# A hybrid decoder layer on one core: the input projection by pairs of column tiles, with the last 128 tokens held still

## The chip, the cores and the metric

The kernel runs on one core of a Trainium2 chip. The metric is device time in microseconds (us) of one launch, as the median of several runs. The engines are named as in the profile: PE is TensorE (PEld its weight loads, which overlap its matmuls), DVE is VectorE, ACT is ScalarE, POOL is GpSimd, and SP is SyncE, which only issues DMAs here. Each engine works through its own instructions in program order; a DMA that an engine issues stands in that order too.

## The reference, cut to what matters

One inference step of a decoder layer for 1024 prompt tokens and 8 x 8 sample tokens, 1088 tokens in all, 2048 features. All tensors are float32.

```
h = x @ w_in + b_in            # (1088 x 2048) @ (2048 x 9984); columns are split into q, k, v, gates
oa = banded_attention(rope(qa), rope(ka), va, window 128, sinks)      # 16 heads
ob = combine over g of banded_attention(rope(q_g), rope(k_g), v_g, dilation 1, 4, 16)   # 8 heads each
ya, yb = oa * silu(za), ob * silu(zb)
m = sigmoid(g_a) * (ya @ w_br_a) + sigmoid(g_b) * (yb @ w_br_b)
y = LayerNorm(alpha * x + m @ w_out)
# also returned: the key/value windows of the prompt and the updated caches of the samples
```

## The kernel before, in words

Every product is made from two float32r parts of each operand, `hi` (the rounded value, a cast on ACT) and `lo` (the rest, a subtraction on DVE): hi x hi, lo x hi and hi x lo, so three matmuls where one stood. `x` is held transposed in the on-chip memory for the whole projection: 16 tiles `xhi[k]`, `xlo[k]` of 128 features x 1088 tokens. The 9984 columns of `w_in` are 78 column tiles of 128.

`in_proj` makes one column tile after the other (the first two together). The weights of a tile are the matmul's stationary side (128 x 128) and the tokens move past them in three chunks, `CHUNKS`, of 384, 384 and 320. For each of four groups of four k-tiles the chunks are taken in turn. That is 16 k x 3 chunks x 3 products = 144 matmuls for a tile, each with a weight load of its own. After its last k a chunk is evacuated by `evac` from PSUM to SBUF with the bias. PSUM has eight banks, four under the tag `d` (`psd()`), where the projection accumulates, and four under `a` (`psa()`), for everything else.

`Weights` loads `w_in` in raw pieces of 512 KB over SP's queue (`wraw`, two buffers), and splits each into two parts of 512 columns (`whi` on ACT, L89; `wlo` on DVE, L90), three parts ahead of the one in use.

The first 34 tiles are q, k and v (`evac_qkv`: rotary on DVE, casts one tick later, stores to DRAM over POOL's queue). The last 44 are the gates z and g (`evac_z`, L954): ACT writes a `z` buffer of which there are two, and SP stores it to DRAM one tick later (L956).

The order of the work beside the matmuls is written by hand: a `tick()` stands after each chunk of a group (12 in a column tile). It first runs what `after(n, f)` had put off, and during the last 44 tiles it then takes a number of steps of a generator, `beside()`: attention (333 steps), decode (111), and `merge` (67), which multiplies the attention results by their weights and by silu(z). `RATES` says how many steps a tick takes in each. In `merge`, an item is one of 12 row tiles of `y`: a step loads `num` (L841, over SP), `w` and `z` (L844, L847, over POOL's queue), DVE multiplies (L854 to L859), ACT takes the sigmoid `sg` (L865), DVE gates (L866, L867), and ACT issues the store of `y` (L890) from the `z` buffer, of which `merge` has two. Items 0 to 7 take 4 steps each, items 8 to 11 take 8. After the projection come the branch and output products (L1019 to L1068), which read `y` back.

Of the kernel before, what the change touches and what calls it, by code (L numbers as in the profile page):

```python
# [10 lines left out]
F32 = mybir.dt.float32  # L11
# [8 lines left out]
P = 128  # L20
# [15 lines left out]
CHUNKS = ((0, 384), (384, 768), (768, T))  # L36
ALPHA = 2.0 ** 0.25
# [14 lines left out]
ORDER = [9] + [n for n, f in enumerate(FT) if f[0] in "qkv" and n != 9]  # L52
ORDER += [n for k in "zg" for n, f in enumerate(FT) if f[0] == k]

# [51 lines left out]
def layer_kernel(ctx: ExitStack, tc: tile.TileContext, A, O, S):  # L106
# [6 lines left out]
    masks = const.tile([P, 4, P], F32, tag="masks", name="masks")  # L113
# [8 lines left out]

    srcs = [tuple(A["w_in"][n, :, 512 * h:512 * (h + 1)] for n in ORDER[:2]) for h in range(4)]
    srcs += [A["w_in"][n, :, 1024 * h:1024 * (h + 1)] for n in ORDER[2:] for h in range(2)]
# [39 lines left out]
    def in_proj(batches, g0, evac, tick):  # L164
        for fts in batches:
            def product(w, i, c, k):
                a, b = CHUNKS[c]
                h, l = (t[:, k % 4 * P:(k % 4 + 1) * P] for t in w)
                o = pts[i][c][:, :b - a]
                nc.tensor.matmul(o, lhsT=h, rhs=xhi[k][:, a:b], start=(k == 0), stop=False)  # L170
                nc.tensor.matmul(o, lhsT=h, rhs=xlo[k][:, a:b], start=False, stop=False)  # L171
                nc.tensor.matmul(o, lhsT=l, rhs=xhi[k][:, a:b], start=False, stop=(k == KT - 1))  # L172

            for kg in range(4):
                if kg == 0:
                    pts = [[psa() if i == 1 and c else psd() for c in range(3)] for i in range(len(fts))]
                if kg == 0 and g0 == 0:

                    ws = [W.get(i) for i in range(2)]
                    g0 = 2  # L180
                    for k in range(4):
                        for i in range(2):
                            for c in range(3):
                                product(ws[i], i, c, k)
                        tick()
                    continue
                for i, ft in enumerate(fts):
                    if g0 < 6:
                        next_x(2)
                        W.load_to(4)  # L190
                    W.ahead(g0)
                    if g0 == 5:
                        constants()
                    w = W.get(g0)
                    g0 += 1
                    for c, (a, b) in enumerate(CHUNKS):
                        for k in range(4 * kg, 4 * kg + 4):
                            product(w, i, c, k)
                        if kg == 3:
                            evac(ft, c, a, b, pts[i][c])  # L200
                        tick()
# [8 lines left out]
    with tc.tile_pool(name="qp", bufs=2, side="right") as qp:  # L210
# [25 lines left out]
        def constants():  # L236
            nc.sync.dma_start(out=bias, in_=A["b_in"])
            for t, n in ((cost, "cost"), (sint, "sint"), (ident, "ident"), (masks, "masks")):
                nc.sync.dma_start(out=t, in_=A[n])
# [10 lines left out]
        for k in range(8):  # L250
            next_x()
            W.split_to((1, 2, 2, 2, 3, 4, 4, 4)[k])
            W.load_to(1 + (k > 1) + (k > 5))
# [12 lines left out]
        def evac_qkv(ft, c, a, b, pt):  # L266
            kind, idx, dil = FT[ft]
            n, e = b - a, min(b, NT)
            m = e - a
            bcol = bias[:, ft:ft + 1]  # L270
            if kind == "v":
                if c == 0:
                    held["f"] = qp.tile([P, T], F32, tag="kv", name="kvf", bufs=3)
                f = held["f"]
# [7 lines left out]
            raw = qp.tile([P, 384], F32, tag="raw", name="raw")  # L282
            sw = qp.tile([P, 384], F32, tag="sw", name="sw")
            nc.scalar.activation(raw[:, :n], pt[:, :n], AF.Identity, bias=bcol)  # L284
            nc.vector.stream_shuffle(sw[:, :n], raw[:, :n], SWAP)
            nc.vector.tensor_mul(raw[:, :n], raw[:, :n], cost[:, a:b])
            nc.vector.tensor_mul(sw[:, :n], sw[:, :n], sint[:, a:b])
            if c == 0:
                held["hi"] = qp.tile([P, NT], F32R, tag="hi", name="qhi", bufs=1)
                held["lo"] = qp.tile([P, NT], F32R, tag="lo", name="qlo", bufs=1)  # L290
                if kind == "k":
                    held["f"] = qp.tile([P, T], F32, tag="kv", name="kvf", bufs=3)
            hi, lo, f = held["hi"], held["lo"], held.get("f")
            if kind == "q":
                nc.vector.tensor_add(raw[:, :n], raw[:, :n], sw[:, :n])  # L295
                src = nat(raw, dil, m)
            else:
                src = cm(f, dil, a, e)
# [4 lines left out]
            def split():  # L303
                nc.scalar.copy(cm(hi, dil, a, e), src)
                nc.vector.tensor_tensor(out=cm(lo, dil, a, e), in0=src, in1=cm(hi, dil, a, e).bitcast(F32),
                                        op=ALU.subtract)
                if e < b:
                    after(3, store)

            def store():  # L310
                if kind == "q":
# [946 lines left out]
```

## Time and profile before

| | us |
|---|---|
| median of 3 runs | 2760.76 |
| lowest, highest | 2759.12, 2764.41 |
| the profiled execution: its own time | 2763.79 |
| the profiled execution: span from first to last instruction | 2761.8 |

The durations below are those of the profiled execution, 3.0 us above the median of the runs. The span holds five stretches: the start (0 to about 20 us), the rest of the q, k and v tiles (to 829 us), the gate tiles with attention and decode beside them (to about 1880 us) and with `merge` beside them (to 2082 us), and the two closing products. A timeline row gives the start, the duration, the engine, the line and the operation; what stands in square brackets is the idle time before it and what ended that.

### The profile page before, as it was taken

The numbers are of one execution on the slowest core, as the hardware profiler recorded it, in microseconds if no ns is written. First come the engines' busy times: TensorE is split into PE (matmuls) and PEld (weight loads), VectorE is DVE, ScalarE is ACT, GpSimd is POOL, SyncE is SP. The second block draws the span as 40 slices with busy tenths as digits, with TensorE's granted clock in tenths as the row PEclk, the third lists the DMA queues.
The fourth block names the chain that finished last, engine by engine and source line by source line (L and its number), as shares of the span: only waits on it lengthen the run. The fifth ranks groups of instructions, "written<-read, shape, count | busy, mean of one in ns | idle before, by whom it ended". The sixth has DMA issues, their size and how long they took to land.

```text
span 2761.8 us, 43516 instructions
## 1 busy us (share of the span) xinstructions
PE 2727.9 (99%) x16643; PEld 2625.8 (95%) x16643; DVE 1477.8 (54%) x2648; ACT 928.5 (34%) x1857; POOL 855.2 (31%) x905
## 2 busy tenths in 40 slices
PE   8999999999999999999999999999999999999997
PEld 8999999999999999999999998889999989988986
DVE  5444442443436777777665432124555556855866
ACT  4122222222223444444433332223224434433442
POOL 1112122131126666677677723433110000000001
PEclk9999999999999999999999999999999999999999
DMA  7345454464464333454445534657876745754763
GB/s 227 102 129 178 161 183 156 142 203 153 161 222 126 113 113 109 129 151 145 145 146 147 149 102 155 198 186 220 277 243 232 245 129 172 235 187 137 244 221 99
DMA packets 206088, 467.64 MB, mean 169 GB/s; under 512 B 28936, under 2 KB 128648, under 8 KB 203128
## 3 DMA queue, kind: packets, MB, share of 16 engines
q1 hardware_dynamic: 167512, 312.33, 35.8%
q0 software_dynamic: 36272, 145.19, 16.7%
q10 hardware_dynamic: 2096, 7.34, 0.7%
q8 instruction: 131, 2.15, 0.3%
q14 instruction: 77, 0.63, 0.1%
HBM read 365.17 MB, written 144.21 MB: 184 GB/s over the span
## 4 chain that ended last, share of the span: by engine, by line
PE 90%; DMA 4%; DVE 4%; ACT 1%; issue 1%; SPq 0%; POOL 0%; ACTq 0%; DVEq 0%; POOLq 0%
PE psd L170 21%; PE psd L172 21%; PE psd L171 21%; PE psd L1064 3%; PE psd L1063 3%; PE psd L1062 3%; PE psa L425 2%; PE psd L1021 2%; PE psd L1020 2%; PE psd L1019 2%; PE psa L487 1%; PE psa L486 1%; PE psa L1064 1%; PE psa L1063 1%; PE psa L1062 1%; PE psa L1021 1%
## 5 line engine op out<-in xcount | busy, mean ns | idle before, releaser
L170 PE MATMUL psd<-xhi,whi 128*128 128x384 f32 (+1 forms) x3712 | 1224.3, 330 | 16.8 <-ACT whi L89 12.3
L172 PE MATMUL psd<-xhi,wlo 128*128 128x384 f32 (+1 forms) x3712 | 1217.5, 328 | 0.5 <-DVE wlo L90 0.4
L171 PE MATMUL psd<-xlo,whi 128*128 128x384 f32 (+1 forms) x3712 | 1216.7, 328 | 0.1
L170 PEld LDWEIGHTS psd<-xhi,whi 128*128 128x128 f32 x3712 | 699.1, 188 | 32.9 <-issue 14.0
L90 DVE TENSOR_TENSOR wlo<-wraw,whi 128x512 fp32r<-128x512 f32 x648 | 449.0, 713 | 478.4 <-ACT whi L89 473.9
L172 PEld LDWEIGHTS psd<-xhi,wlo 128*128 128x128 f32 x3712 | 698.6, 188 | 2.0 <-DVE wlo L90 2.0
L171 PEld LDWEIGHTS psd<-xlo,whi 128*128 128x128 f32 x3712 | 699.1, 188 | 0.4 <-DVE xlo L226 0.4
L89 ACT CAST whi<-wraw 128x512 fp32r<-128x512 f32 x648 | 386.7, 618 | 393.2 <-PE psa L1063 151.7
L460 POOL PARTITION_ALL_REDUCE md<-s x160 | 310.1, 1938 | 67.2 <-ACT s L457 44.0
L446 POOL PARTITION_ALL_REDUCE md<-s x160 | 214.4, 1340 | 177.5 <-DVE s L435 65.0
L1126 POOL DMA_DIRECT2D o_y<-h x24 | 13.0, 542 | 573.0 <-DVE h L994 562.4
L477 DVE TENSOR_TENSOR pl<-s,ph 128x512 fp32r<-128x512 f32 (+1 forms) x160 | 128.0, 800 | 100.3 <-ACT ph L476 98.3
L1062 PE MATMUL psd<-whi,m 128*128 128x512 f32 x384 | 149.8, 390 | 0.5 <-ACT whi L89 0.5
L1063 PE MATMUL psd<-whi,m 128*128 128x512 f32 x384 | 149.8, 390 | 0.0
L1064 PE MATMUL psd<-wlo,m 128*128 128x512 f32 x384 | 149.7, 390 | 0.0
L457 ACT ACTIVATE s<-s 128x256 f32<-128x256 f32 (+1 forms) x160 | 75.9, 475 | 196.2 <-DVE s L456 196.0
L954 ACT ACTIVATE z<-psd,bias 128x384 f32<-128x384 f32 x132 | 73.8, 562 | 191.9 <-PE psd L172 126.2
L312 POOL DMA_DIRECT2D s_sq<-raw x20 | 11.5, 576 | 371.9 <-DVE raw L295 371.9
L1021 PE MATMUL psd<-y,wlo 128*128 128x384 f32 (+1 forms) x384 | 125.7, 327 | 0.1
L1019 PE MATMUL psd<-y,whi 128*128 128x384 f32 (+1 forms) x384 | 125.4, 326 | 0.0
L1020 PE MATMUL psd<-y,whi 128*128 128x384 f32 (+1 forms) x384 | 125.4, 326 | 0.0
L284 ACT ACTIVATE raw<-psd,bias 128x384 f32<-128x384 f32 (+1 forms) x79 | 44.2, 559 | 199.4 <-PE psd L172 199.4
(209 smaller groups left out, 3314.4 us busy)
## 6 DMA issues: line engine op xcount, KB each, us to landing
wraw<-w_in SPq DMA_DIRECT2D x152, 512.0 KB
wraw<-w_out SPq DMA_DIRECT2D x96, 512.0 KB
wraw<-w_br SPq DMA_DIRECT2D x72, 512.0 KB
o_c<-c POOLq DMA_DIRECT2D x64, 510.0 KB, 8.5
qst<-s_qs SPq DMA_DIRECT2D x80, 256.0 KB
s_zg<-z SPq DMA_DIRECT2D x64, 192.0 KB
kv<-ktb POOLq DMA_DIRECT2D x48, 256.0 KB, 3.7
kv<-vb POOLq DMA_DIRECT2D x48, 256.0 KB, 3.2
```

What stands on the lines that cost most here:

```text
L89: self.nc.scalar.copy(hi, raw)
L90: self.nc.vector.tensor_tensor(out=lo, in0=raw, in1=hi.bitcast(F32), op=ALU.subtract)
L170: nc.tensor.matmul(o, lhsT=h, rhs=xhi[k][:, a:b], start=(k == 0), stop=False)
L171: nc.tensor.matmul(o, lhsT=h, rhs=xlo[k][:, a:b], start=False, stop=False)
L172: nc.tensor.matmul(o, lhsT=l, rhs=xhi[k][:, a:b], start=False, stop=(k == KT - 1))
L446: nc.gpsimd.partition_all_reduce(u["md"][:, 0], top, P, RED.max)
L460: nc.gpsimd.partition_all_reduce(u["md"][:, 1], s[:, 1 if n == 1 else 2], P, RED.add)
L1019: nc.tensor.matmul(o, lhsT=h, rhs=yt[k][:, 0, :n], start=st, stop=False)
L1021: nc.tensor.matmul(o, lhsT=l, rhs=yt[k][:, 0, :n], start=False, stop=en)
L1062: nc.tensor.matmul(pt, lhsT=h, rhs=whi, start=st, stop=False)
L1063: nc.tensor.matmul(pt, lhsT=l, rhs=whi, start=False, stop=False)
L1064: nc.tensor.matmul(pt, lhsT=h, rhs=wlo, start=False, stop=en)
```

## The change

The column tiles are taken in 39 pairs (`PAIRS`: v or k with a q, then q with q, then gates with gates), and `w_in` is laid out by pairs on the host. For the first 960 tokens the weights are still the stationary side, and the tokens move in chunks of 512 and 448 (`ICH`). For the last 128 tokens the sides are swapped: `x` is the stationary side and the 256 weight columns of the pair move past it (`still`), so that the result lies with tokens on the partitions. At the end of a pair ACT copies it out, PE transposes it in two 128 x 128 blocks, and it is evacuated as the third chunk of each tile.

A pair has eight groups of two k-tiles with three ticks each, 24 in a pair, as before. All four `d` banks belong to the pair in work, and one `a` bank to `still`. The first loop takes 18 pairs (the first pair of gates among them), the second 21.

```diff
+ICH = ((0, 512), (512, 960), (960, T))
...
+    def in_proj(pairs, g0, evac, tick, temp):
+        for fts in pairs:
+            pts = [[psd() for _ in range(2)] for _ in range(2)]
+            acc = psa()
+            for kg in range(8):
...
+                W.ahead(g0)
+                hi, lo = W.get(g0)
...
+                def still(kk):
+                    k = 2 * kg + kk
+                    h, l = (t[:, 2 * kk * P:(2 * kk + 2) * P] for t in (hi, lo))
+                    xh, xl = (x[k][:, ICH[2][0]:] for x in (xhi, xlo))
+                    o = acc[:, :2 * P]
+                    nc.tensor.matmul(o, lhsT=xh, rhs=h, start=(k == 0), stop=False)
+                    nc.tensor.matmul(o, lhsT=xl, rhs=h, start=False, stop=False)
+                    nc.tensor.matmul(o, lhsT=xh, rhs=l, start=False, stop=(k == KT - 1))
+
+                if kg < 7:
+                    moving(0, 0, 0), moving(0, 0, 1), moving(0, 1, 0)
+                    tick()
+                    moving(0, 1, 1), moving(1, 0, 0), moving(1, 0, 1)
+                    tick()
+                    moving(1, 1, 0), moving(1, 1, 1), still(0), still(1)
+                    tick()
                     continue
+                still(0), still(1)
+                t = temp()
+                nc.scalar.copy(t, acc[:, :2 * P])
+                moving(0, 0, 0), moving(0, 0, 1)
+                tick()
+                pt = psa()
+                for i in range(2):
+                    nc.tensor.transpose(pt[:, P * i:P * (i + 1)], t[:, P * i:P * (i + 1)], ident)
+                moving(0, 1, 0), moving(0, 1, 1)
+                evac(fts[0], 2, *ICH[2], pt[:, :P])
+                moving(1, 0, 0)
+                tick()
+                moving(1, 0, 1)
+                moving(1, 1, 0), moving(1, 1, 1)
+                evac(fts[1], 2, *ICH[2], pt[:, P:2 * P])
+                tick()
...
-            raw = qp.tile([P, 384], F32, tag="raw", name="raw")
-            sw = qp.tile([P, 384], F32, tag="sw", name="sw")
+                st["raw"] = qp.tile([P, T], F32, tag="raw", name="raw")
+            sw = qp.tile([P, 512], F32, tag="sw", name="sw", bufs=1)
...
-            after(1, split)
+            after((11 if ft in SECOND else 3) + c, split)
...
         def at_scores(u):
...
-            u["v"] = once(("v", u["kv"], u["lo"], u["hi"]), lambda: load_v(u))
...
         def at_split(u):
             s, n = u["s"], len(u["kbs"])
+            u["v"] = once(("v", u["kv"], u["lo"], u["hi"]), lambda: load_v(u))
...
-                nc.sync.dma_start(out=num[:, :n], in_=S["num"][i + 4 * g, :, :n])
+                nc.gpsimd.dma_start(out=num[:, :n], in_=S["num"][i + 4 * g, :, :n])
...
-                        nc.scalar.dma_start(out=S["y"][i], in_=zs[i])
+                        after(1, lambda z=zs[i], i=i: nc.scalar.dma_start(out=S["y"][i], in_=z))
...
-            z = zp.tile([P, 384], F32, tag="z", name="z")
+            z = zp.tile([P, 512], F32, tag="z", name="z")
...
-RATES = (1.0, 1.15, 0.9)
+RATES = (1.06, 1.15, 0.95)
```

The first place is PE in the middle of the projection. Before, in one column tile, the weights `whi` and `wlo` of one tile meet a chunk k by k; the number behind `xhi` is the k-tile.

```order
L170 MATMUL psd_2231<-xhi7_155,whi_2156 128x384
L171 MATMUL psd_2231<-xlo7_156,whi_2156 128x384
L172 MATMUL psd_2231<-xhi7_155,wlo_2157 128x384
L170 MATMUL psd_2232<-xhi4_126,whi_2156 128x320
L171 MATMUL psd_2232<-xlo4_127,whi_2156 128x320
L172 MATMUL psd_2232<-xhi4_126,wlo_2157 128x320
```

Now, at the end of the first pair, the last `moving` of a group, `still` of that group and of the next, and the transposes (L223) behind two more k-tiles of the first bank:

```order
L193 MATMUL psd_530<-xhi13_323,whi_694 128x448
L194 MATMUL psd_530<-xlo13_324,whi_694 128x448
L195 MATMUL psd_530<-xhi13_323,wlo_695 128x448
L204 MATMUL psa_531<-whi_694,xhi12_317 128x256
L205 MATMUL psa_531<-whi_694,xlo12_318 128x256
L206 MATMUL psa_531<-wlo_695,xhi12_317 128x256
```

```order
L206 MATMUL psa_531<-wlo_734,xhi15_365 128x256
L193 MATMUL psd_527<-xhi14_361,whi_733 128x512
L194 MATMUL psd_527<-xlo14_362,whi_733 128x512
L195 MATMUL psd_527<-xhi14_361,wlo_734 128x512
L193 MATMUL psd_527<-xhi15_365,whi_733 128x512
L194 MATMUL psd_527<-xlo15_366,whi_733 128x512
L195 MATMUL psd_527<-xhi15_365,wlo_734 128x512
L223 MATMUL psa_833<-ident_64,still_817 128x128 x2
L193 MATMUL psd_528<-xhi14_361,whi_733 128x448
```

The 320-token chunk is gone; its first 64 tokens moved into wider chunks, and the other 128 (with the rest of the second chunk) into `psa`, 256 columns for two tiles.

The second place is ACT during attention. Before, the three evacuations `z` of a column tile stand one tick apart, with the attention's own work (`s`, `ph`, `pvl`) and the weight casts (`whi`) between them:

```order
L89 CAST whi<-wraw 128x512
L954 ACTIVATE z<-psd,bias 128x384
L457 ACTIVATE s<-s 128x512
L476 CAST ph<-s 128x256
L954 ACTIVATE z<-psd,bias 128x384
L490 COPY pvl<-psa 64x256
L954 ACTIVATE z<-psd,bias 128x320
```

Now, at the end of a pair:

```order
L218 COPY still<-psa 128x256
L998 ACTIVATE z<-psd,bias 128x512
L534 COPY pvl<-psa 64x256
L998 ACTIVATE z<-psd,bias 128x448
L998 ACTIVATE z<-psa,bias 128x128
L500 ACTIVATE s<-s 128x512
L520 CAST ph<-s 128x256
L998 ACTIVATE z<-psd,bias 128x512
L998 ACTIVATE z<-psd,bias 128x448
L998 ACTIVATE z<-psa,bias 128x128
```

Six evacuations now stand in the last three ticks of 24, and none in the other 21; the two `z` buffers are as before, each wider.

The third place is `merge`. Before, SP's queue has the `num` loads among the weight loads and the stores of `z`:

```order
L956 DMA s_zg<-z 128x320
L841 DMA num<-s_num 128x1088
L78 DMA wraw<-w_in 128x1024
L841 DMA num<-s_num 128x1088
L78 DMA wraw<-w_in 128x1024
L956 DMA s_zg<-z 128x384
```

Now they head each item's loads on POOL's queue (L888 and L891 are the old L844 and L847, L848 belongs to the weights of the combination), and SP has weights and `z` alone there:

```order
L848 DMA m<-s_md 8x16x16 x2
L885 DMA num<-s_num 128x1088
L888 DMA w<-s_wa 64x1024 x2
L891 DMA z<-s_z 128x1088
L848 DMA m<-s_md 8x16x16 x2
```

POOL's queue lost nothing and gained the 544 KB of `num` (512 KB for the later groups of an item) ahead of each `w` and `z`; the order among the others is the same.

## Rows read from the trace of the kernel before

**Rows 1.** The page: PE's part of the busy times, and the chain that ended last.

```profile
PE 2727.9 (99%) x16643; PEld 2625.8 (95%) x16643; DVE 1477.8 (54%) x2648; ACT 928.5 (34%) x1857; POOL 855.2 (31%) x905
...
PE 90%; DMA 4%; DVE 4%; ACT 1%; issue 1%; SPq 0%; POOL 0%; ACTq 0%; DVEq 0%; POOLq 0%
```

**Rows 2.** Busy us of each engine (x instructions) by stretch; then clock, DMA share, GB/s.

```profile
0.00:20.00 20.00, 12.46 (x50) 11.32 (x51) 7.57 (x7) 8.19 (x9) 0.19 (x4) 1.00 0.75 243
...
860.00:1600.00 740.00, 740.00 (x4767) 740.00 (x4766) 528.30 (x986) 319.49 (x706) 509.12 (x312) 1.00 0.45 133
1880.00:2050.00 170.00, 160.31 (x953) 158.51 (x952) 95.02 (x110) 42.67 (x74) 41.65 (x77) 0.98 0.86 265
...
2600.00:2762.00 162.00, 146.47 (x703) 123.61 (x701) 106.04 (x171) 57.96 (x108) 11.64 (x10) 0.96 0.53 174
```

**Rows 3.** Timeline, ACT: the last evacuation of a q tile, and twelve tiles later.

```profile
87.73 0.53 ACT L284 ACTIVATE raw<-psd,bias 128x320 f32<-128x320 f32 x1
...
373.33 0.52 ACT L284 ACTIVATE raw<-psd,bias 128x320 f32<-128x320 f32 x1
```

**Rows 4.** Timeline, PE: matmuls of 512 columns in `out_proj`, 100 starts apart.

```profile
2290.00 0.39 PE L1063 MATMUL psa<-whi,m 128*128 128x512 f32 x1
...
2312.67 0.39 PE L1064 MATMUL psa<-wlo,m 128*128 128x512 f32 x1
```

**Rows 5.** Timeline, PE: matmuls of 384 columns in `in_proj`, nine starts apart.

```profile
400.52 0.34 PE L170 MATMUL psd<-xhi,whi 128*128 128x384 f32 x1
...
402.08 0.34 PE L170 MATMUL psd<-xhi,whi 128*128 128x384 f32 x1
```

**Rows 6.** Timeline, PE: eight attention matmuls of 256 columns, each with new weights.

```profile
1104.11 0.28 PE L486 MATMUL psa<-ph,vst 128*128 128x256 f32 x1
...
1105.07 0.34 PE L170 MATMUL psd<-xhi,whi 128*128 128x384 f32 x1
```

**Rows 7.** Timeline, PE: four transposes between matmuls, and the boundary behind the q, k, v tiles.

```profile
422.61 0.60 PE L341 MATMUL psa<-ident,kvf 128*128 128x128 f32 x4
422.97 0.39 PE L170 MATMUL psd<-xhi,whi 128*128 128x320 f32 x1
423.20 0.30 PE L171 MATMUL psd<-xlo,whi 128*128 128x320 f32 x1
...
828.39 0.66 PE L341 MATMUL psa<-ident,kvf 128*128 128x128 f32 x4 [0.78 <-ACT kvf L275]
```

**Rows 8.** ACT: a PSUM copy, an evacuation of z; its waits for z buffers, 1600 to 1880.

```profile
998.93 0.37 ACT L434 COPY s<-psa 128x256 f32<-128x256 f32 x1
1000.63 0.53 ACT L954 ACTIVATE z<-psd,bias 128x320 f32<-128x320 f32 x1 [1.32 <-PE psd L172]
...
ACT z L954 <- DMA s_zg<-z: 4.4, 2, 2.9
```

**Rows 9.** DVE in 300 us of attention: busy time (x), and its longest wait (us, times, longest).

```profile
880.00:1180.00 300.00, 238.32 (x459) 1.00 0.39 115
...
DVE pl L477 <- ACT ph L476: 40.6, 58, 0.8
```

**Rows 10.** Timeline, ACT's queue: the stores of y of items 0, 7 and 11.

```profile
1900.51 0.37 ACTq L890 DMA_DIRECT2D s_y<-z  x1
...
1969.41 0.33 ACTq L890 DMA_DIRECT2D s_y<-z  x1
...
2052.35 0.33 ACTq L890 DMA_DIRECT2D s_y<-z  x1
```

**Rows 11.** In `merge`: SP's timeline, ACT's timeline, and PE's waits from 1880 to 2050.

```profile
1964.35 18.73 SPq L841 DMA_DIRECT2D num<-s_num  x3
...
1993.92 0.53 ACT L954 ACTIVATE z<-psd,bias 128x320 f32<-128x320 f32 x1 [15.51 <-DMA s_zg<-z]
...
PE psd L170 <- ACT whi L89: 5.2, 1, 5.2
PE psd L170 <- ACT z L954: 4.4, 2, 2.5
```

More of the change, by code (lines that the diff above doesn't have):

```diff
@@ L51 @@
 FT += [("z", 8 + i, 1) for i in range(4)] + [("g", i, 1) for i in range(32)]
-ORDER = [9] + [n for n, f in enumerate(FT) if f[0] in "qkv" and n != 9]
-ORDER += [n for k in "zg" for n, f in enumerate(FT) if f[0] == k]
+_Q, _K, _V = ([n for n, f in enumerate(FT) if f[0] == k] for k in "qkv")
+_KV = [n for kv in zip(_V, _K) for n in kv]
+PAIRS = [(n, _Q[i]) for i, n in enumerate(_KV)]
+PAIRS += [(_Q[i], _Q[i + 1]) for i in range(len(_KV), len(_Q), 2)]
+_Z = [n for k in "zg" for n, f in enumerate(FT) if f[0] == k]
+PAIRS += [(_Z[i], _Z[i + 1]) for i in range(0, len(_Z), 2)]
+SECOND = [n for _, n in PAIRS]
+FIRST = 18
 class Weights:
@@ L162, in layer_kernel @@
     xhi, xlo = [], []
[L164 to L185, printed above, removed]
-                    continue
[L187 to L201, printed above, removed]
@@ L237, in constants @@
             nc.sync.dma_start(out=bias, in_=A["b_in"])
[L238 removed]
+            for t, n in ((cost, "cost"), (sint, "sint"), (ident, "ident")):
                 nc.sync.dma_start(out=t, in_=A[n])
@@ L267, in evac_qkv @@
             kind, idx, dil = FT[ft]
+            if kind == "z":
+                z = qp.tile([P, T], F32, tag="kv", name="z", bufs=3)[:, :b - a]
+                nc.scalar.activation(z, pt[:, :b - a], AF.Identity, bias=bias[:, ft:ft + 1])
+                after(1, lambda: nc.gpsimd.dma_start(out=S["z"][idx, :, a:b], in_=z))
+                return
             n, e = b - a, min(b, NT)
@@ L307, in split @@
                 if e < b:
-                    after(3, store)
+                    after(1, store)
             def store():
+                hi, lo = st["hi"], st["lo"]
                 if kind == "q":
@@ L375, in tick_q @@
                 nc.gpsimd.dma_start(out=O[f"c{g}"][b, r:e], in_=A[f"c{g}"][b, NQ + r:NQ + e])
-        in_proj([ORDER[:2]] + [[ft] for ft in ORDER[2:34]], 0, evac_qkv, tick_q)
+        in_proj(PAIRS[:FIRST], 0, evac_qkv, tick_q,
+                lambda: qp.tile([P, 2 * P], F32, tag="sv", name="still", bufs=2))
         while later or copies:
@@ L386, in attention @@
         ap = pool.__enter__()
+        masks = ap.tile([P, 4, P], F32, tag="masks", name="masks", bufs=1)
+        nc.sync.dma_start(out=masks, in_=A["masks"])
         def once(key, f):
@@ L933, in layer_kernel @@
     ypool = gp = nxt = None
-    rest = ORDER[34:]
-    end = now[0] + 12 * len(rest)
+    rest = PAIRS[FIRST:]
+    end = now[0] + 24 * len(rest)
     bg = Beside(beside(), 1.0)
@@ L956, in evac_z @@
             after(1, lambda: nc.sync.dma_start(out=dst, in_=z[:, :b - a]))
-        in_proj([[ft] for ft in rest], 34 * 4, evac_z, tick_rest)
+        in_proj(rest, 8 * FIRST, evac_z, tick_rest, lambda: zp.tile([P, 2 * P], F32, tag="still", name="still", bufs=1))
         while later:
```

65 lines of the change are left out of this document (42 added, 23 removed).

## The prediction

> **What bounds the kernel now.** I read the page first: PE is busy 99% of the span, and the chain that ended last is PE for 90% [rows 1]. Time therefore goes in two ways only, through the number and spacing of matmuls and through the stretches in which PE stands. The sums by stretch show where it stands [rows 2]: 7.5 us of the first 20, nothing in attention, 9.7 us beside `merge` (170 less 160.31), 15.5 us at the very end. The projection is most of the span: twelve column tiles take 373.33 - 87.73 = 285.6 us, 23.80 us each [rows 3], and 78 of them with what runs beside them are the first 2082 us.
>
> Matmuls overlap, so their durations mislead; what counts is from start to start. With 512 columns that is 22.67/100 = 0.2267 us [rows 4], with 384 it is 1.56/9 = 0.1733 [rows 5], with 256 and new weights every time 0.96/8 = 0.120 [rows 6]. From 384 to 512 each column costs 0.0534/128 us = 0.417 ns, which is the 2.4 GHz level, and the granted clock reads 1.00 in attention [rows 2]. What is left, 0.2267 - 512 x 0.000417 = 0.0133 us, goes with the matmul and not with its columns. The 256-column row lies on the same line (0.1067 + 0.0133 = 0.120), so the weight load does not show even there.
>
> **The change, part by part.** *Columns and matmuls.* A pair streams as many columns as before: 2 x 1088 x 48 = 104,448, against 2 x 960 x 48 + 256 x 48. Matmuls fall from 288 to 240, and 48 x 0.0133 = 0.64 us. Two transposes are added: four of them took 0.36 us, and the 320-column matmul behind them 0.23 instead of 0.147 (384 less 64 columns), so 0.11 us each, 0.22 a pair [rows 7]. That leaves 0.42 us saved per pair. Counted from whole tiles it is more: 47.60 before, and after 96 x (0.2267 + 0.2000) + 48 x 0.120 + 0.22 = 46.94, 0.66 saved; 448 columns are 512 less 64. The two counts differ because a tile of 23.80 us is 0.12 longer than its spacings add up to (48 x 0.4933 = 23.68), and I cannot see whether the new pair keeps that. I take the middle, 0.54 us, for 39 pairs **-21**, bounds -16 and -26.
>
> A rule speaks against this term. The Trainium skill ("TensorE: Matmul & The Clock Gate", section "Back-to-back issue gap") gives an isolated gap of N/2.4 + 2.5 ns when the clock is full. By it 512 columns would take 0.2158 us where this trace has 0.2267 [rows 4], and 48 matmuls fewer would give back only 0.12 us, less than the transposes take; the measured rows decide, and the sum stays as it is.
>
> *The copy of `still`.* ACT takes about 0.37 us [rows 8]; PE has six 512-column matmuls, 1.36 us, before the transposes ask for it. It costs nothing while ACT is less than a microsecond late; without that cover every further microsecond falls on PE once a pair.
>
> *Six evacuations at the end of a pair.* Let T be the end of the first bank. Then follow 0.22 of transposes and 1.20 + 1.36 + 1.20 us of matmuls, and the next pair wants the banks back at T + 4.0, 5.3, 6.5 and 7.9. An evacuation of 512 columns will take some 0.65 us (320 took 0.53 [rows 8]). With s from the end of an evacuation to the landing of its store, two `z` buffers in turn give: the third evacuation ends at T + 0.95 + s, the fourth at T + 2.7 + s, the fifth, which waits for the third's store, at T + 1.6 + 2s. The last is late when s exceeds 3.15 us, by 2 us for each us of s. Before, a buffer came round after two ticks, 3.97 us less 0.58, and ACT waited for one only twice from 1600 to 1880, 4.4 us in all [rows 8]; so s is mostly under 3.4 there. Per pair that is 0 to 0.5 us, over the some 18 pairs beside attention and decode 0 to 9: I take **+2**, as it is nearer to no waits. One PSUM bank fewer for attention is in the same bound.
>
> *Rates.* An attention unit is two steps and eight 256-column matmuls: before 2 x 1.983 + 0.96 = 4.93 us (a tick is 23.80/12), after 2 x 1.955/1.06 + 0.96 = 4.65. DVE was busy 238.3 us of 300 and waited 40.6 for a cast that nothing can fill [rows 9]; over 300/4.93 = 61 units that is 4.57 us each. It fits by 0.08 us. I count nothing, and 5 us at the high end (under 2% of the some 330 us).
>
> *`merge`.* From the store of item 0 to that of item 7 it took 68.9 us, from there to item 11 82.9 [rows 10], together 151.8. In ticks it had 7 x 4/0.9 + 4 x 8/0.9 = 66.7, or 132.2 us; it fell behind by 19.6, PE stood for 9.7 of it [rows 2], and 9.9 were carried past the end. The new rate gives it 7 x 4/0.95 + 4 x 8/0.95 = 63.2 ticks of 1.955 us, 123.5 us. At its own old pace it is 28.3 behind, and with the same 9.9 carried PE stands 18.4: +8.7. What limits the pace is partly the DMA queues, busy 0.86 with 265 GB/s [rows 2], whose bytes do not change. Partly it is SP: one run of `num` loads held it 18.73 us, with weights and a `z` store behind them, ACT then waited 15.5 us for that store, and PE for ACT's casts and evacuations [rows 11]. That blocking goes away. If items 8 to 11 then take 17 us instead of 20.7, PE stands 3.6 (-6). If instead `z`, now behind `num` on POOL's queue, costs items 0 to 7 1.5 us each, +19. I take **+8**: pair ends let ACT fall behind by only 4 us before PE feels it. The store of `y`, a tick later, waits less on ACT and frees its buffer later; I put it at nothing within these bounds.
>
> *The rest.* At 828.39 the transposes of the last v tile waited 0.78 us [rows 7]; v is no longer last: **-1**. In the start x arrives at the pace of the loads before and after; the second k-tile is now asked for after three matmuls instead of nine, but fewer are left to do when it comes: 0, bounds -1.5 and +1.5. The later casts and whole-tile buffers of the q, k, v loop lie under PE, since a store has 8 ticks (16 us) before its buffer is rewritten and weights are split three parts ahead (3 x 5.9 us); if that cover went, the first wait would be PE's on `whi`. `load_v` moves two units later with two units to go.
>
> The sum on the profiled execution's own 2763.8: -21 + 2 + 8 - 1 = -12, 2751.8. It lies 3.0 above the median of the runs, on whose scale that is 2748.8, say 2749.
>
> **The rivals.** *Merge gives nothing back* (with SP free of `num`): -21 - 6 + 1 - 1 = -27, 2734. For it speaks SP's 18.73 us [rows 11], against it the DMA share of 0.86. *No change*: merge takes +19 and evacuations +2: -1, 2760. For it, POOL's queue gets 544 KB more per item on some 1060, and `merge` was already 19.6 us behind at a slower rate [rows 10]. *Slower, by the `z` buffers*: at the ends of the 21 gate pairs PE waits for the fourth bank. From -12 it takes 17.5 us to reach +5.5, 0.83 us a pair, s = 3.6 us. A store now carries a third more bytes than the one that took under 3.4; at s = 4.2 it is 2.1 us a pair, 44 us, and 2791. Against it: before 1600 no such wait is seen. *The fixed part does not go with the matmul*: if the swapped matmuls or the wide chunks cost 0.0133 us more each than the line says, only the transposes are left, +8.6 for 39 pairs, and 2749 + 21 + 9 = 2779; rows 4 and 6 both lie on the line, so it is unlikely. The skill's gap formula above is a milder form of it.
>
> **How the numbers follow.** A difference under 0.2%, 5.5 us, can hardly be told from none in this kernel. Chances: the forecast, 2740 to 2757, 0.52; merge gives nothing back, 2728 to 2740, 0.17; no change 0.18; the `z` buffers 0.09; the fixed part 0.04. Below 2755.3 lie 0.48 of the forecast, the first rival and 0.06 of "no change": faster 0.71. Same is the rest of these two and a little of the `z` buffers, 0.17; slower the last two less that, 0.12. The range runs from 2734, where the first rival has its time (half of its 0.17 lies below), to 2764, which takes in "no change" with 5 us of attention on top: 2734 to 2764 leaves out about 2 in 10.
>
> **What would show it.** Right: 240 matmuls a pair, starts 0.227, 0.200 and 0.120 us apart, a pair in 46.9 to 47.2 us without work beside it; PE's idle time beside `merge` 12 to 25 us, at pair ends, ended by ACT's evacuations or casts; no `num` on SP. Wrong: a pair over 47.4 (the fixed part); waits of PE for ACT's `z` at every pair end of attention, with ACT waiting for `s_zg` (the buffers); PE waiting for DVE in attention (the rates); or PE never standing beside `merge`.

## The result, and the profile after

The changed kernel takes 2835.4 us, median of four runs (2834.0 to 2842.6), against 2761.4 for the kernel before: 1.0273 of its time (95% interval 1.0260 to 1.0287), 74 us slower, and 86 us over the forecast. The profiled execution took 2834.0 us, its span 2832.2.

The page of the changed kernel: busy times, and the chain that ended last.

```profile
PE 2744.3 (97%) x14849; PEld 2403.3 (85%) x14849; DVE 1464.2 (52%) x2648; ACT 939.7 (33%) x1896; POOL 867.2 (31%) x931
...
PE 72%; DVE 10%; DMA 8%; ACT 4%; issue 4%; POOL 1%; SPq 0%; ACTq 0%; DVEq 0%; POOLq 0%
```

Against [rows 1] PE issues 1794 instructions fewer and is yet busy 16 us longer, and 28% of the chain now runs through others than PE, where it was 10%.

Busy us of each engine by stretch of the changed kernel (columns as in [rows 2]):

```profile
110.00:390.00 280.00, 278.25 (x1426) 244.43 (x1425) 97.81 (x207) 60.05 (x120) 66.30 (x120) 1.00 0.49 161
390.00:889.00 499.00, 489.09 (x2492) 428.49 (x2491) 199.92 (x396) 122.57 (x218) 102.67 (x188) 1.00 0.48 162
889.00:1600.00 711.00, 693.92 (x3876) 617.16 (x3874) 500.26 (x948) 299.88 (x672) 480.61 (x300) 1.00 0.44 127
...
1915.00:2149.00 234.00, 202.99 (x1062) 175.08 (x1061) 107.42 (x134) 58.71 (x108) 54.97 (x102) 0.94 0.73 224
```

PE now stands in the q, k, v loop (11.7 us in the first two rows), in attention (17.1, none before [rows 2]) and beside `merge` (31.0). Busy time hides short gaps, since a matmul in flight covers them. So I also took, from start to start, all that exceeds the spacing of a matmul's size (waits, and matmuls that run at the lower clock right behind one: after the wait of 7.17 us shown further down the granted clock is 0.50, the 1.2 GHz level, and 448 columns are 0.37 us apart where 0.2025 is usual). In decode, with its small matmuls of many sizes, the figure is rough.

| stretch | lost before, us | lost after, us |
|---|---|---|
| start, 100 us | 5.1 | 4.8 |
| q, k, v loop | 1.0 | 14.1 |
| attention, to 1600 | 0 | 26.8 |
| decode, to 1880 and 1915 | 29.0 | 27.0 |
| `merge`, to 2082 and 2149 | 13.0 | 39.6 |
| closing products | 1.7 | 5.8 |

The sums are 49.8 and 118.1: 68 of the 70 us between the spans are lost in this way. The pairs themselves gave nothing, as the clean pair below shows.

PE's waits in the changed kernel (us in all, times, longest):

```profile
PE psa L223 <- ACT still L218: 31.3, 9, 10.8
PE psd L193 <- ACT raw L324: 11.7, 5, 2.5
PE psd L193 <- ACT whi L99: 7.5, 2, 6.2
PE psa L531 <- DVE pl L521: 4.1, 7, 0.8
PE psd L193 <- ACT z L998: 3.7, 4, 1.7
```

Three of these lines are new kinds of wait: the transposes for the copy of `still`, the first matmul of a pair for an evacuation into `raw`, the values of attention for `pl`. Timeline of PE in a pair of two q tiles, one group of two k-tiles from its first start to that of the next, and the copy of `still` on ACT at the ends of pairs two apart:

```profile
769.60 0.39 PE L193 MATMUL psd<-xhi,whi 128*128 128x512 f32 x1
...
774.83 0.28 PE L204 MATMUL psa<-whi,xhi 128*128 128x256 f32 x1
...
775.51 0.39 PE L193 MATMUL psd<-xhi,whi 128*128 128x512 f32 x1
```

```profile
740.67 0.37 ACT L218 COPY still<-psa 128x256 f32<-128x256 f32 x1 [6.08 <-PE psa L206]
...
835.85 0.37 ACT L218 COPY still<-psa 128x256 f32<-128x256 f32 x1 [6.08 <-PE psa L206]
```

A pair in which nothing stands takes 95.18/2 = 47.59 us. Two tiles took 2 x 23.80 = 47.60 before [rows 3]. Twelve matmuls of 512 and twelve of 448 columns take 774.83 - 769.60 = 5.23 us where the prediction had 12 x 0.4267 = 5.12. Over the whole projection 512 columns are 0.2325 us apart on average, 448 are 0.2025, 256 in `still` 0.1166, and 384 in the kernel before 0.1748: each time 0.452 to 0.456 ns a column.

### The profile page after: what moved, and what is told of

Read it like the earlier page. It is cut to its first block, busy times and chain, and to the rows that moved or that the text cites. A ratio compares the mean times of both kernels' runs of the same rounds, so it can differ in the third digit from the quotient of the medians.

```text
span 2832.2 us, 40009 instructions
## 1 busy us (share of the span) xinstructions
PE 2744.3 (97%) x14849; PEld 2403.3 (85%) x14849; DVE 1464.2 (52%) x2648; ACT 939.7 (33%) x1896; POOL 867.2 (31%) x931
## 4 chain that ended last, share of the span: by engine, by line
PE 72%; DVE 10%; DMA 8%; ACT 4%; issue 4%; POOL 1%; SPq 0%; ACTq 0%; DVEq 0%; POOLq 0%
PE psd L193 14%; PE psd L194 14%; PE psd L195 14%; PE psd L1106 3%; PE psd L1108 3%; PE psd L1107 3%; DMA s_zg<-z 2%; PE psd L1063 2%; PE psd L1064 2%; PE psd L1065 2%; PE psa L204 2%; PE psa L206 2%; PE psa L205 2%; DVE s L499 2%; ACT ph L520 2%
## 5 line engine op out<-in xcount | busy, mean ns | idle before, releaser
L193 PE MATMUL psd<-xhi,whi 128*128 128x512 f32 x2496 | 965.0, 387 | 23.4 <-ACT raw L324 11.7
L194 PE MATMUL psd<-xlo,whi 128*128 128x512 f32 x2496 | 953.1, 382 | 0.5 <-DVE xlo L256 0.5
L195 PE MATMUL psd<-xhi,wlo 128*128 128x512 f32 x2496 | 951.0, 381 | 0.9 <-DVE wlo L100 0.9
L193 PEld LDWEIGHTS psd<-xhi,whi 128*128 128x128 f32 x2496 | 472.4, 189 | 105.0 <-ACT raw L324 13.5
L195 PEld LDWEIGHTS psd<-xhi,wlo 128*128 128x128 f32 x2496 | 471.9, 189 | 77.2 <-DVE wlo L100 2.1
L194 PEld LDWEIGHTS psd<-xlo,whi 128*128 128x128 f32 x2496 | 472.8, 189 | 65.4 <-DVE xlo L256 1.6
L204 PE MATMUL psa<-whi,xhi 128*128 128x256 f32 x624 | 174.8, 280 | 0.0
L206 PE MATMUL psa<-wlo,xhi 128*128 128x256 f32 x624 | 174.3, 279 | 0.0
L205 PE MATMUL psa<-whi,xlo 128*128 128x256 f32 x624 | 174.1, 279 | 0.0
```

The source lines that it names most:

```text
L204: nc.tensor.matmul(o, lhsT=xh, rhs=h, start=(k == 0), stop=False)
L205: nc.tensor.matmul(o, lhsT=xl, rhs=h, start=False, stop=False)
L206: nc.tensor.matmul(o, lhsT=xh, rhs=l, start=False, stop=(k == KT - 1))
```

## The experiments

Every kernel is the changed one with the edit shown, unless it says "before". The edits are cut to what they change, and some of their lines are put in words. Times are medians, to be read against 2835.4; those of the kernel before and the last two runs are read against the kernel before as it was timed beside them, 2759.4 to 2762.5.

### Does anything go with a matmul?

**Halves.** Each moving 512 as two of 256 on the same weights.

```diff
+for u, v in ((0, 256), (256, 512)) if b - a == 512 else ((0, b - a),):
+    ou = o[:, u:v]
     ... three matmuls into ou, rhs[:, a + u:a + v]
```

> The changed kernel with every moving matmul of 512 columns in the projection made as two of 256 columns on the same weights: 96 more matmuls in each of the 39 pairs, the same columns. Theory P (in this loop a moving matmul costs its columns, about 0.455 ns each, and nothing goes with the matmul): two of 256 take 2 x 116.6 ns for the 232.5 ns of one of 512, a clean pair stays at 47.5 us, and the time stays at 2835 us within 6. Rival F (what the prediction used: 13.3 ns go with every matmul, and the wide chunks lose some 6 ns for another reason): two of 256 take 2 x 120 ns, 7.5 ns more 96 times in 39 pairs, 28 us, so 2863 us; with the full 13.3 ns it is 50 us, 2885.

2844.9 us, +9.4. The copy of `still`, two pairs apart as above:

```profile
748.17 0.37 ACT L221 COPY still<-psa 128x256 f32<-128x256 f32 x1 [6.17 <-PE psa L209]
...
843.80 0.37 ACT L221 COPY still<-psa 128x256 f32<-128x256 f32 x1 [6.17 <-PE psa L209]
```

95.63/2 = 47.82 us a pair, 0.225 more for 96 matmuls more: here 2.3 ns goes with a matmul, not 13.3. Theory P holds but for these 2.3 ns, which make 9 us over 39 pairs and so put the time 4 us above its range; F asked for at least 0.72 us a pair.

**Order of the products.**

```diff
-h xhi, h xlo, l xhi
+h xhi, l xhi, h xlo
```

> The changed kernel with the three products of a moving chunk in another order, the one of the last product of the kernel: high weights on high x, low weights on high x, high weights on low x, so that the same x moves twice in a row. Theory O (the order is why 512 columns take 232.5 ns here and 227 there): 512 columns fall to 227 ns and 448 to 199, 0.9 us per clean pair, 46.6 to 46.8 us, and the time by 25 to 35 us, 2800 to 2810 us. Rival N (the order does not matter; what the difference is from stays open): a clean pair stays at 47.5 us, 2832 to 2840 us.

2838.1 us: no gain, N. Why 512 columns are 0.2325 us apart in the projection and 0.227 in `out_proj` stays open.

**The last 128 tokens move too.** Per k-tile six matmuls of 128 columns on the tiles' own weights in place of three of 256; no copy, no transposes.

```diff
-xh, xl stationary, h and l of both tiles (256 columns) moving
+for i in range(2): h, l of tile i stationary, xh, xl (128 columns) moving
```

> The changed kernel without the swap of operands: the last 128 tokens move past the weights in chunks of 128 columns, six matmuls instead of three for each k-tile, into the two halves of the same bank; no copy, no transposes. Theory P (columns set the pace, 0.455 ns each and some 2 ns with each matmul): a clean pair of k and q stays at 47.4 to 47.9 us, PE's waits for still (31 us) go and with them the loss in attention, 2800 to 2815 us. Rival W (at 128 columns the load of the next weights shows: 70 ns and more instead of 58): 1.1 us or more per clean pair, 45 us, which eats that gain: 2840 us or more.

2992.6 us. Rival W, far beyond its bound. Timeline of PE, eleven starts:

```profile
804.39 0.27 PE L206 MATMUL psa<-xlo,whi 128*128 128x128 f32 x1
...
805.62 0.44 PE L193 MATMUL psd<-xhi,whi 128*128 128x512 f32 x1
```

1.23/11 = 0.112 us for 128 columns, almost what 256 take. The price by columns ends there, and a pair takes 52.4 us. So without the swap chunks of 512 and 448 would cost 4.8 us a pair. Before, a chunk of 320 avoided narrow matmuls, and two tiles took what a pair takes now.

### The q, k, v loop

**A raw buffer for k.**

```diff
-st["raw"] = qp.tile([P, T], F32, tag="raw", name="raw")
+st["raw"] = qp.tile([P, T], F32, tag="raw" if kind == "q" else "rawk", name="raw", bufs=2 if kind == "q" else 1)
```

> The changed kernel with a buffer of its own for the raw tile of a k, so that the q behind it in the pair no longer takes the buffer that the k has just used. Theory R (at five ends of a pair of k and q ACT stands up to 6 us until DVE has finished the k, and PE then waits 2.1 to 2.9 us for the first bank): these five waits go, 12 to 14 us less, 2822 us, and no wait of PE for the evacuation into raw is left. Rival D (DVE itself is late with that chain, and the next thing that needs it, the weights' low parts or the next pair's evacuation, takes the wait over): 2829 to 2837 us, with PE's waits under another name.

2824.2 us, -11.2, and PE's waits for `raw` are gone: theory R. In the changed kernel, at the end of a pair of k and q (timeline of DVE, then of ACT):

```profile
496.88 1.10 DVE L334 TENSOR_TENSOR kvf<-raw,sw 128x512 f32<-128x512 f32 x1
...
502.09 0.22 DVE L336 TENSOR_TENSOR kvf<-raw,sw 128x64 f32<-128x64 f32 x1
```

```profile
502.40 1.21 ACT L324 ACTIVATE raw<-psd,bias 128x512 f32<-128x512 f32 x2 [6.04 <-DVE kvf L336]
```

In five of the seven pairs of k and q the q gets the buffer that its own pair's k has just used. ACT's evacuation waits until DVE has rotated all three chunks of the k, and PE up to 2.5 us for the bank. Before, a tile's chunks came a tick of 2 us apart, and the next tile's first came 20 us after the last.

### The transposes

**At the end of the pair.**

```diff
-pt = psa(); transposes after moving(0, 0, *); each evacuation of chunk 2 behind two products
+pt = psa(); for i in range(2): transpose(i); evac(fts[i], 2)   # after the last product
```

> The changed kernel with the two transposes and the two evacuations behind them moved to the very end of the pair, so that some 5 us of matmuls instead of 1.4 lie between the copy of still and the transposes. Theory S (PE's round trip through ACT's queue in the middle of a pair's end is what stands: 31.3 us in nine waits, most of them beside merge): 18 to 28 us less, 2807 to 2817 us, and PE's waits for still under 10 us. Rival A (ACT is blocked so long, for a z load or a z buffer, that PE waits as long one step later, at the banks of the next pair or for its weights): 2828 to 2838 us, with the waits moved to the first matmul of a pair.

2907.1 us. The edit brought a wait of its own, by PE's list:

```profile
PE psa L228 <- ACT z L997: 93.0, 21, 12.5
PE psa L228 <- ACT raw L323: 8.7, 10, 0.9
```

The second transpose writes the bank that ACT is reading for the first evacuation. With both transposes first:

```diff
+for i in range(2): transpose(i)
+for i in range(2): evac(fts[i], 2)
```

> The transposes at the end of the pair as in the run before, but both of them ahead of both evacuations: there the second transpose had to wait until ACT had read the first one's half of the bank, and that wait was the edit's own. Theory S (the round trip of PE through ACT's queue stands, and 5 us of matmuls cover what 1.4 did not): PE's 31.3 us of waits for still fall under 12, 18 to 28 us less than the changed kernel, 2807 to 2817 us. Rival A (ACT is blocked so long that PE waits one step later): 2828 to 2840 us, the waits at the first matmuls of a pair.

2823.0 us, -12.5, between the two ranges; PE's waits for `still` fall to 9.2 us in three, as S has it. But the time does not come from there. The copy of `still` in the seventeenth pair and in the last, in this kernel, then with the raw buffer alone and the transposes where they were, then (the last only) in the changed kernel:

```profile
826.51 0.37 ACT L218 COPY still<-psa 128x256 f32<-128x256 f32 x1 [6.09 <-PE psa L206]
...
2133.11 0.37 ACT L218 COPY still<-psa 128x256 f32<-128x256 f32 x1 [6.09 <-PE psa L206]
```

```profile
827.06 0.37 ACT L218 COPY still<-psa 128x256 f32<-128x256 f32 x1 [6.08 <-PE psa L206]
...
2133.15 0.37 ACT L218 COPY still<-psa 128x256 f32<-128x256 f32 x1 [6.08 <-PE psa L206]
```

```profile
2143.91 0.37 ACT L218 COPY still<-psa 128x256 f32<-128x256 f32 x1 [6.08 <-PE psa L206]
```

In the changed kernel the seventeenth stands at 835.85 (above). So 9.3 of the 10.8 us are gained in the q, k, v loop, where the waits for `raw` are gone in this run too: with the third chunks last, the q asks for its buffer before the k has given its own back. Behind the loop 1.5 us are gained, no more than with the raw buffer alone (2.0). So the 22 us of waits for `still` are lost again elsewhere, as A has it, in part under other names: `whi` 10.5, `pl` 5.7, `wlo` 4.8 us, where they were 7.5, 4.1 and 0.9.

### Attention

**The rates of before** (and `y` stored at once, as `merge` ends later).

```diff
-RATES = (1.06, 1.15, 0.95)
+RATES = (1.0, 1.15, 0.9)
```

> The changed kernel with the rates of before (1.0, 1.15, 0.9), and y stored at once as before. Theory V (the higher rate of attention asks more of DVE and ACT than they have, so PE waits for probabilities, values and still there, 24 us from 889 to 1600 us more than before): these waits fall by 12 to 20 us, 2815 to 2823 us; what merge has to catch up at its end may cost 5 of it. Rival E (the waits in attention come from the bursts at the pair ends and stay whatever the rate): 2831 to 2840 us, with waits from 889 to 1600 us at 20 or more.

2824.1 us, -11.3, a microsecond above V's range. Lost in attention: 3.8 us for 26.8, a larger fall than theory V asked for; beside `merge`, which now lacks ticks, 54 for 40.

**Before, with the new rates.**

```diff
-RATES = (1.0, 1.15, 0.9)
+RATES = (1.06, 1.15, 0.95)
```

> The kernel before with the rates of the changed one alone (1.06 and 0.95 for 1.0 and 0.9). Theory V (the rate is what costs PE 23 us in attention, whatever the pairs): 12 to 24 us more there, some of it given back by merge, which has more time: 2766 to 2782 us, with waits of PE for pl, num and the banks between 830 and 1600 us. Rival B (the rate costs only together with the pairs, whose six evacuations and copy of still come in a burst): within 6 us of before or, as merge has more time, up to 10 less, 2751 to 2767 us.

2766.9 us, +4.6 (1.0013 to 1.0035 of its time). The time lies in both ranges; the waits decide for rival B. Busy times from 889 to 1600 us, in this kernel, then with the old rates in the changed one:

```profile
889.00:1600.00 711.00, 711.00 (x4588) 711.00 (x4587) 502.90 (x952) 308.91 (x681) 496.56 (x314) 1.00 0.47 137
```

```profile
889.00:1600.00 711.00, 709.50 (x3988) 635.57 (x3987) 505.72 (x944) 303.46 (x676) 474.43 (x295) 1.00 0.44 130
```

PE never stands in the first; where the 4.6 us are was not followed up. So in attention the rate costs only together with something that the pairs bring.

**A buffer for the small evacuations.**

```diff
-z = zp.tile([P, 512], F32, tag="z", name="z")
+z = zp.tile([P, 512], F32, tag="z", name="z") if c < 2 else zp.tile([P, P], F32, tag="z2", name="z2", bufs=1)
```

> The changed kernel with a buffer of its own for the 128-column evacuations of the gate tiles, so that the two of 512 columns serve four evacuations of a pair instead of six. Theory Z (the z buffers are what blocks ACT at the ends of pairs): ACT's 36 us of waits for stores from 889 to 1600 us fall under 20, PE's loss there from 27 us under 15, and the time by 10 to 18 us, 2817 to 2825 us. Rival T (it is the copy of still, that stands in ACT's queue behind attention's work and that PE waits for): within 6 us of 2835.

2806.1 us, -29.4, the largest gain of one edit, beyond theory Z. ACT's waits for stores from 889 to 1600, in the changed kernel and in this one:

```profile
ACT z L998 <- DMA s_zg<-z: 24.5, 17, 2.4
...
ACT z L998 <- DMA s_z<-z: 11.2, 9, 2.2
```

```profile
ACT z L998 <- DMA s_zg<-z: 9.7, 8, 2.1
ACT z L998 <- DMA s_z<-z: 2.2, 3, 0.9
```

Lost in attention: 5.6 us for 26.8 at the new rate. The bursts through two buffers are what the rate does not bear. At the old rate ACT waits just as long for the stores (39.8 us) and PE does not stand.

**Stores of z at once.**

```diff
-after(1, lambda: nc.sync.dma_start(out=dst, in_=z[:, :b - a]))
+nc.sync.dma_start(out=dst, in_=z[:, :b - a])
```

> The changed kernel with the stores of the gate tiles issued at once instead of a tick later, so that a z buffer comes free up to 2 us sooner. Theory Z (six evacuations through two buffers are a good part of the loss: ACT waits 36 us for these stores in attention and 26 beside merge, and everything behind them on ACT is late): 10 to 20 us less, 2815 to 2825 us, with ACT's waits for stores halved. Rival Y (these waits of ACT lie under PE's work; SP, which now waits for ACT at the store, delays loads instead): 2830 to 2842 us.

2845.9 us, +10.5, above both ranges. ACT waits 37.8 us for stores in attention, 35.7 without the edit: asking sooner did not free a buffer sooner. SP stood before these stores for ACT's `z` either way, 69.7 us there and 69.2 without the edit. What the 10 us are was not followed up.

### Beside merge

**Before, with num on POOL's queue and y a tick later; and num alone.**

```diff
-nc.sync.dma_start(out=num[:, :n], in_=S["num"][i + 4 * g, :, :n])
+nc.gpsimd.dma_start(out=num[:, :n], in_=S["num"][i + 4 * g, :, :n])
```

> The kernel before with one part of the change alone: merge loads num on POOL's queue instead of SP's, and y is stored a tick later. Theory M (z and the weights now stand behind num on POOL, so merge itself gets slower): PE's time without work beside merge grows from 13 us to 20 or more, 2768 to 2778 us. Rival S (SP is free of num, and merge gains as the prediction's first rival had it; what the changed kernel lost there comes from its round trip through ACT and from having less time): 3 to 8 us less than before, 2754 to 2759 us.

> The kernel before with num on POOL's queue and y stored at once, as before. Theory N (num is what costs: z and weights stand behind it on POOL): 2770 to 2776 us as with both edits. Rival Y (the later store of y costs, since it frees the z buffer a tick later): 2758 to 2765 us.

2774.1 and 2778.2 us, +12 and +16: it is `num` (M, N); the later `y` costs nothing. POOL's longest wait in the second, from 1880 us:

```profile
POOL num L841 <- DVE w L858: 58.7, 7, 12.4
```

POOL stands before `num` until DVE has used up the one buffer, and `w` and `z` stand behind it in the queue, whatever their own buffers do. Before, POOL stood about as long (54.6 us), but at `w` itself. DVE's waits for `w` from 1880 to 2090 us, before and in the second:

```profile
DVE w L858 <- DMA w<-s_wb: 10.3, 2, 6.5
...
DVE num L854 <- DMA w<-s_wa: 2.4, 2, 1.8
```

```profile
DVE w L858 <- DMA w<-s_wb: 40.9, 7, 10.0
...
DVE num L854 <- DMA w<-s_wa: 24.0, 5, 11.9
```

The wait on SP held other loads [rows 11], and that blocking did go: ACT's longest wait for a gate tile's store falls from 15.5 to 5.3 us, its waits for raw weights from 23.0 to 4.3. On POOL the wait holds merge's own loads, and that costs more. In the changed kernel the trip through ACT meets merge's waits: timeline of ACT, then of PE.

```profile
1960.93 0.33 ACTq L934 DMA_DIRECT2D s_y<-z  x1
1971.78 0.66 ACT L909 ACTIVATE sg<-z 128x544 f32<-128x544 f32 x1 [11.88 <-DMA z<-s_z]
1972.34 0.60 ACT L99 CAST whi<-wraw 128x512 fp32r<-128x512 f32 x1
1972.96 0.37 ACT L218 COPY still<-psa 128x256 f32<-128x256 f32 x1
```

```profile
1973.39 0.69 PE L223 MATMUL psa<-ident,still 128*128 128x128 f32 x2 [7.17 <-ACT still L218]
```

ACT waits 11.88 us for a z, the copy stands two instructions behind, and PE 7.17 us for it. Whether `num` made this z late is not shown.

**num on SP again.**

```diff
-nc.gpsimd.dma_start(out=num[:, :n], ...)
+nc.sync.dma_start(out=num[:, :n], ...)
```

> The changed kernel with num loaded on SP's queue again, nothing else. Theory M: of the 39.6 us that PE loses from 1915 to 2149 us some 12 to 20 go, 2815 to 2823 us. Rival S: the loss stays or grows, since SP then holds the z stores and weights behind num: 2833 to 2842 us.

2827.0 us, -8.5: the direction of M, less than it asked for. ACT's longest wait for a z load is still 12.2 us, and PE waits 25.3 us for `still` where it waited 31.3.

### Together

**Raw buffer, old rates, 17 pairs first** (`FIRST = 17`); then with `num` on SP, `y` at once and late transposes too; then with four ticks more ahead of attention and the `z2` buffer.

> The changed kernel with a raw buffer for k (as in the second run), the rates of before, and 17 pairs instead of 18 in the first loop, so that 44 tiles lie beside attention, decode and merge as before and merge ends in time with its old rate. Theory V (the rates are what PE loses in attention, raw what it loses ahead of it, and two tiles more beside give merge its time back): 2835 - 11 - 23 - 10 to 15 for merge, 2786 to 2794 us. Rival E (merge loses as much whatever its time, since ACT waits for z and DVE waits for ACT): 2800 to 2810 us.

> Everything that has helped so far, put together on the changed kernel: a raw buffer for k, transposes at the end of the pair, the rates of before with 17 pairs in the first loop, num on SP's queue and y stored at once. Theory C (the losses are separate and the pairs themselves gain nothing): 2802 - 8 for num - 9 for still, 2781 to 2788 us, still 20 us above the kernel before. Rival G (the pairs do gain the 16 to 26 us of the prediction once nothing else stands): 2745 to 2762 us. Rival M (the waits beside merge only change their name): 2793 to 2803 us.

> The combined kernel with attention started four ticks later, so that its first q has landed, and with the buffer of its own for the 128-column evacuations. Theory C (what is left are waits with names): 8 to 12 us less than 2795, 2783 to 2787 us. Rival M (merge ends that much later and PE waits there instead): 2791 to 2798 us. Neither expects it under the kernel before, 2762.

2801.9, 2794.8 and 2811.5 us. The first two lie in the ranges of E and M, the third above both of its ranges, so the sums were too hopeful. One reason: with 17 pairs SP stands before the load of `masks`, which the change moved into attention's pool. By SP's list from 800 to 850 us of the second:

```profile
SPq L430 <- DVE sw L327: 32.2, 1, 32.2
```

Attention's first q and the weights stand behind it, and PE lost 7.2 us there. Starting attention later therefore changed only the name of that wait (`whi`, 6.3 us). In the third ACT also waited longer for stores of gate tiles in attention, 45.3 us for 37.1, though it has a buffer more; the last two runs show why.

**Three mends on the changed kernel: raw, z2, num on SP; and the same with late transposes.**

> The changed kernel with three mends: a raw buffer for k, a buffer of its own for the 128-column evacuations of gates, num on SP's queue. Rates, 18 pairs and the later y as in the changed kernel. Theory C (the losses are separate): 2835 - 11 - 29 - 8, 2784 to 2790 us. Rival M (merge has the time that attention gives back taken again, since it waits for loads): 2792 to 2800 us.

> The same with the transposes at the very end of the pair. Theory S (PE's round trip through ACT still costs beside merge): another 6 to 12 us less, 2775 to 2782 us. Rival A (with the z buffers mended ACT answers in time, or is so late that PE waits one step later): within 4 us of the run with three mends. The kernel before stays ahead in both cases, 2762.

2779.5 and 2815.6 us. Three mends give 55.9 of the 74 us, more than their sum of 49 and 4 us below C's range, but stay at 1.0072 (1.0053 to 1.0091) of before. Late transposes cost 36 us here, which neither theory had: by ACT's list from 889 to 1600 us

```profile
ACT z L998 <- DMA s_zg<-z: 24.9, 14, 3.1
ACT z L998 <- DMA s_z<-z: 13.7, 7, 3.7
```

both small evacuations now come one behind the other into the one `z2` buffer, so the wait for a store is back (38.6 us, 9.3 with three mends), and PE stands there for 16.9 us instead of 3.6. The second and third kernels of this section have the late transposes too. What is left with three mends is PE's list from 1900 us:

```profile
PE psa L223 <- ACT still L218: 14.3, 3, 8.8
PE psd L193 <- ACT z L998: 0.9, 1, 0.9
```

No version that I ran beats the kernel before.

## Why the prediction was wrong

**"Columns and matmuls", -21: measured about 0.** This is the step that set the sign. "What is left, 0.0133 us, goes with the matmul and not with its columns" drew a line through 512 columns of `out_proj` [rows 4] and 384 of `in_proj` [rows 5], two loops. The line itself is no accident. In the branch products of the kernel before, which are one loop, 384 columns and then 320 lie on it as well (timeline of PE, 99 starts apart each):

```profile
2100.16 0.34 PE L1019 MATMUL psa<-y,whi 128*128 128x384 f32 x1
...
2117.32 0.34 PE L1019 MATMUL psd<-y,whi 128*128 128x384 f32 x1
...
2562.23 0.31 PE L1019 MATMUL psd<-y,whi 128*128 128x320 f32 x1
...
2576.75 0.31 PE L1019 MATMUL psd<-y,whi 128*128 128x320 f32 x1
```

That is 0.1733 and 0.1467 us, again 0.417 ns a column and 0.0133 us besides. But the projection does not keep to it: there the price is by the column, 0.452 to 0.456 ns at each size from 256 to 512, and the halves put 2.3 ns on a matmul. The nine starts of [rows 5], 0.1733, hid that; the mean of their loop is 0.1748, which is also the 0.12 us a tile that the prediction could not place. By these spacings the matmuls of a pair take 96 x (0.2325 + 0.2025) + 48 x 0.1166 = 47.36 us, 0.24 less than two tiles before, and the two transposes (0.22 in the prediction) take that back. The rival "the fixed part does not go with the matmul" got 0.04 and was right on this, and its sign, a pair over 47.4, came: 47.59. The Trainium skill ("TensorE: Matmul & The Clock Gate", section "Back-to-back issue gap") has 2.5 ns for this part; the halves agree with that, while its N/2.4 is too fast here: 0.455 ns a column, not 0.417. The prediction set the rule aside since its sum for 512 columns missed the row, and dropped with it the part that was right.

**"Six evacuations at the end of a pair", +2: 20 to 29.** The formula looked at PE's banks, and rightly so little stands there (3.7 us for `z`). What stood was ACT, 35.7 us in attention, and behind it on ACT the `still` copy and attention's own casts. The rival by the `z` buffers had the cause and a size (2791 us), but the wrong place of the wait; 0.09 was too little.

**"Rates", 0, at most 5: 23, together with the buffers.** "It fits by 0.08 us" left nothing for the bursts. Either mend alone takes away over 20 us, so the two terms are one loss and must not be added; the rate alone costs the kernel before no wait.

**"The copy of `still`", nothing while ACT is less than a microsecond late.** The condition was named, but no price was put on it though [rows 11] showed ACT 15.5 us late. PE waits 31.3 us for the copy. With more matmuls ahead of the transposes it waits 9.2, and the time gains nothing beyond what the raw buffer gives: the waits mark how late ACT is, for reasons of its own, and PE meets them at the copy or elsewhere.

**"`merge`", +8: some 27.** "That blocking goes away" was right of SP, but the price on POOL was set too low and in the wrong place: `num` there costs the kernel before 12 to 16 us alone, within my upper bound (+19) but not my value. I had put it on items 0 to 7. With `num` alone on POOL it takes 69.5 us from the store of item 0 to that of item 7, for 68.9, and 94.8 from there to item 11, for 82.9 [rows 10]. In the changed kernel `num` on SP gives 8.5 back; what the rest is was not separated.

**"Later casts and whole-tile buffers lie under PE", 0: 11 to 13.** The argument counted when a buffer is rewritten after its store, and not which tile gets it: in a pair of k and q the q asks for the buffer within a microsecond of the k's last chunk being put into it.

Right were the start (4.8 us lost for 5.1), the transposes of v, for which PE no longer waits, and the absence of `num` on SP. By the losses of the table (21 for the columns, 13 for the loop, 25 and 19 above what I had for attention and merge, 4 in the closing products) 82 of the 86 us between forecast and result have a place. The 4 us in the closing products I did not follow up.

## What to carry to other kernels

Take a per-instruction price from two sizes in the loop that is to be changed, or by splitting one of its instructions in two; a price that holds in the closing products made a gain out of nothing in the projection. When work is gathered into bursts, count the buffers and the in-order queues that the burst passes, and look at what else stands behind it there: ACT's 36 us of waits cost PE nothing at one rate and over 20 us at 6% more. A new trip from PE through another engine and back meets every wait that this engine has anyway. Moving the trip moved the waits and saved no time; buffers for what made the engine late did. And when an edit gives time back, look at where in the run it does: the late transposes seemed to mend the trip, and had mended a buffer in another stage.

## What the hardware showed unexpectedly

In the projection, with new weights of 128 x 128 for each matmul, a moving 128 columns take 0.112 us and 256 take 0.117: from 256 down to 128 the price hardly falls, from 256 to 512 it goes with the columns at 0.452 to 0.456 ns. In the closing products of the same kernel it is 0.417 ns a column and 0.0133 us a matmul (0.1467, 0.1733 and 0.2267 us for 320, 384 and 512 columns), at a granted clock of 1.00 in both. The order of products is not why, and the cause is open.
